# A hybrid encoder layer on one core: VectorE and ScalarE in source order in all stages

## The chip, the cores and the metric

The kernel runs on one core of a Trainium2 chip. Five engines with a queue of instructions each take part: TensorE (PE, matrix products), VectorE (DVE, elementwise work), ScalarE (ACT, activations, copies and casts), GpSimd (POOL) and SyncE (SP, which issues most of the DMA transfers). The metric is the device time of one execution in microseconds, lower is better. The kernel before took 1963.14 us, the median of three runs between 1960.15 and 1968.09.

## The reference

One encoder layer on a sequence of 1024 tokens of width 1024, all in float32. Each of three sub-layers is normalised ahead and behind (sandwich RMSNorm):

```
x += 1/2 * post(SwiGLU_1(pre(x)))                 # silu(x Wg) * (x Wu), then Wd; width 2816
x += post(W_out [ norm(NA heads) | norm(dilated heads) ])
x += 1/2 * post(SwiGLU_2(pre(x)))
```

The middle one has a combined projection to q, k and v for 16 heads of 64 elements. Eight heads do neighbourhood attention on a 16 x 64 grid of tokens, with a learned relative bias; eight do a mixture of three dilated sliding windows (128, 512 and 2048 wide, dilations 1, 4 and 16), merged with weights from the softmax denominators.

## The kernel before

**Products.** Each float32 operand is split into a high and a low part: ScalarE casts (`nc.scalar.copy(hi, raw)`, line 344) and VectorE subtracts (line 345). `mm3` (lines 251 to 253) makes one product of three TensorE passes, high by high, high by low, low by high. The GEMMs for gate and up (both FFNs) and for query and key are done by a scheme with seven products of half-size blocks (Winograd's form of Strassen's), named A11, A12, S2, S1, S3, S4 and A22 in the code. One product of a block is 12 matmuls. The down projections and the values take another form of the same scheme, in seven passes (`Passes`, with its own splits in lines 601 and 602). The output projection is plain.

**The loop of blocks.** `PairGemm.run` handles one block b of the weights per turn: 22 blocks in an FFN, 8 for query and key. For the first blocks (`early`: 9 in the first FFN, 10 in the second, all 8 for query and key) A11 and A12 were done in a phase before, `ahead`, and five products are left. In the source the turn of an early block holds, in this order:

- product S2, and VectorE adds u2 (line 470);
- the tail of the block before, `last()`: product A22, VectorE's c21 (line 507), the split of B22 (344 and 345, in `rest`), then the sink's work: Silu (554) and a product (555) for gate and up, and for every second block four more VectorE operations (563 to 566); for query and key `put`, which scales (806) and casts (808) on ScalarE and subtracts (809) on VectorE;
- the preparation of the next block's weights: `direct` (three VectorE operations, lines 432 to 434, ahead of them a split of the left weights where the next block isn't early) and `second` (the split of T2);
- product S1, and VectorE's v (line 478), which reads the bank of S1;
- product S3, c22 (line 499), the split of T1;
- product S4, which adds into the bank that v has read, and the sink's `second`.

A late block does all seven products. There s1, u2 and v are copies by ScalarE (line 363, in `keep`), the sink's `first` (VectorE's add 526, Silu 528) follows product A12, and `direct`, `second`, S1 and v follow that.

**What sets the order.** The instructions of a stage are handed to a scheduler. Within `ordered(*more)` it keeps TensorE in the order of the source, and the engines given as `more` too; for the others it chooses an order by its own costs. Before the change only the first stage (the first norm and the first products, up to `order.close()` in `begin`, line 1341) names VectorE and ScalarE. `c.behind(f, engines)` asks that f's instructions on these engines come no earlier than their place in the source. SP and POOL, and with them most DMA issues, are ordered by the scheduler everywhere.

**Three regions** follow the first stage: from line 1342 on, the rest of the first FFN, the value passes and query and key; from 1454, attention (`DilPair.head` and `na_head`) with parts of the output projection as fillers; from 1495, the output projection, its norms and the second FFN.

Of the kernel before, what the change touches and what calls it, by code (L numbers as in the profile page):

```python
# [16 lines left out]
SP, POOL, DVE, ACT = [getattr(mybir.EngineType, e) for e in ("SP", "Pool", "DVE", "Activation")]  # L17
# [822 lines left out]
def q_by_residue(c, copy, st):  # L840
    q = c.op.tile([P, SEQ], F32R, tag="q", name="q")
    by_residue(copy, q, st[:, 0])
    return q
# [264 lines left out]
def layer(tc, a, out):  # L1108
    nc = tc.nc
    c = Ctx(tc)  # L1110
    with ExitStack() as ctx:
        def pool(name, bufs, stack=ctx, **kw):
            return stack.enter_context(tc.tile_pool(name=name, bufs=bufs, reuse_waits="tile", **kw))

        def sub():
            return ctx.enter_context(ExitStack())
# [5 lines left out]
        def ordered(*more):  # L1122
            return tc.manual_schedule(engines={mybir.EngineType.PE, *more})
# [147 lines left out]
        def load_head():  # L1271
            if not heads:
                return
            p, hd = heads.pop(0)
            st = load_stack(c, p, hd)
            if hd == 0:
                pairs[p] = DilPair(c, p, attended if p == 2 * NP - 1 else lambda: None) if p >= NP else na_v(c, p)
            loaded.append((pairs[p], st, pairs[p].bias(hd) if p >= NP else na_bias(c, p, hd)))
# [15 lines left out]
        with ExitStack() as order:  # L1294
# [4 lines left out]
            def load(ts, queues):  # L1299
                for t, q in zip(ts, queues):  # L1300
                    xs[t] = c.xp.tile([P, D], F32, tag="x", name="x", bufs=4)
                    q.dma_start(xs[t], x0[t])
# [4 lines left out]
            def begin(pg):  # L1307
                load((2, 3), (nc.scalar, nc.sync))

                def drain():  # L1310
                    while c.sums:
                        c.sums.popleft()()

                def norm(*ts):
                    op0.scale(*n[ts])
                    drain()
                def junk():
                    return c.xp.tile([P, D], F32, tag="s", name="junk", bufs=2)
                n = {(0, 1): op0.squares([0, 1], [xs[0], xs[1]], junk())}
                norm(0, 1)  # L1320
                pg.split_left(0)
                n[2, 3] = op0.squares([2, 3], [xs[2], xs[3]], junk())
                op0.one(0)
                op0.one(1)
                pg.split_left(1)
                acc, s1 = [pg.bank() for _ in range(2)], []
                for b in range(2):
                    pg.mm(acc[b], pg.w[b], 0, A11, cols=slice(0, 256))
                op0.one(0)
                norm(2, 3)  # L1330
                op0.one(2)
                op0.one(3)
                for b in range(2):
                    pg.mm(acc[b], pg.w[b], 0, A11, cols=slice(256, 512))
                    s1.append(pg.save(b, acc[b]))
                    if b:
                        op0.one(1)
                load((4, 5), (nc.gpsimd, nc.gpsimd))
                op0.one(2)
                op0.one(3)  # L1340
                order.close()
                order.enter_context(ordered())
                return s1
            F = lambda *ts: lambda: op0.norm(ts, [xs[t] for t in ts])
            L, U = (lambda *ts: lambda: load(ts, [nc.gpsimd] * 2)), (lambda t: lambda: op0.put(t))
# [103 lines left out]
        def most():  # L1449

            early.extend(GroupNorm(c, og[0], 4 * quad, gd[:, :512], True, None) for quad in range(2))
            for n in early:
                c.todo.append(lambda n=n: c.behind(lambda: n.squares(slice(0, 448), 0), ACT))
        with ordered():
            ops = sub()
            c.op = pool("op", 2, ops)
            c.vp.append(c.op)
            load_head()
            qs = deque()

            def next_ready():

                if loaded:
                    d, st, g = loaded[0]
                    if isinstance(d, DilPair):
                        qs.append(q_by_residue(c, nc.gpsimd.tensor_copy, st))
                        by_residue(nc.gpsimd.tensor_copy, g[:, 0], g[:, 2])
                    else:
                        nc.gpsimd.tensor_add(g[:, 1], g[:, 0], c.cmask)
            c.behind(lambda: qs.append(q_by_residue(c, nc.scalar.copy, loaded[0][1])), ACT)  # L1470
            for p in range(NP, 2 * NP):
                for hd in range(2):
                    d, st, g = next_head()
                    if hd == 0:
                        d.outputs()
                    d.head(hd, st, qs.popleft(), g, next_ready, (1, 0) if p > NP or hd else (0, 1))
            c.left = 64
            for p in range(NP):
                for hd in range(2):
                    vs, st, nb = next_head()  # L1480
                    if (p, hd) == (NP - 1, 1):
                        c.todo.extend([lambda: None, most])
                    na_head(c, p, hd, og[0], vs, st, nb, next_ready, last if (p, hd) == (NP - 1, 1) else lambda q: None)
            c.last_units()
            c.fill(len(c.fillers))
            c.tick(len(c.todo))
            on = [c.xt.tile([P, 2, 4, T], F32R, tag=f"o{h}", name=f"n{h}") for h in (0, 2)]
            for n in early:
                n.ot = on
                c.steps.extend(lambda i=i, n=n: n.put(i) for i in range(4))  # L1490
# [1 line left out]

        s6 = sub()
        c.psm = pool("psm", 6, s6, space=PSUM)
        with ordered():
            part, ws, od = [xo[k] for k in ("part", "ws", "dil")]
            held = [nat_bank(c) for _ in range(4)]
            for t in range(4):
                for k in range(4):
                    nat_mm(c, held[t], od[1], t, k, ws, True, False)  # L1500
                    if t > 1 or k % 2:
                        c.step()
            c.flush()
            s4.close()
            s3.close()
            s2.close()
            c.xa = pool("xa", 1, side="right")
            prep = sub()
            hs1p = pool("hs1", 1, prep, side="right")
            p2, g3 = prep_pool(prep, [(a["mix_post_g"], "post"), (a["ffn2_pre_g"], "pre")])  # L1510
            left_pool(prep, side="right")
            op = Operand(c, g3, 2)
            pg = gate_pairs(3, op, a["wg2"], a["wu2"], 10)
            fin = Finish(c, x1, x2, p2, op)
            hs = [part, hs1p.tile([P, 4, D], F32, name="hs")]
            A = lambda *ts: lambda: fin.rest(ts, lambda t: hs[t // 4][:, t % 4, :])
            U = lambda t: lambda: op.put(t)

            def sink(h, t, g, ps):
                cols = slice(g * T, (g + 1) * T)  # L1520
                to = hs[h][:, t, cols]
                if h == 0:
                    nc.vector.tensor_add(to, ps, to)
                    ps = to
                sumsq(c, ps, fin.ss[:, 4 * h + t, g:g + 1])
                nc.vector.tensor_mul(to, ps, p2[:, cols])
                c.tick()
            for g in (1, 0):
                ws = nat_weights(c)
                for t in range(4):  # L1530
                    acc = nat_bank(c)
                    nat_chain(c, acc, on[0], t, ws, True, True)
                    sink(0, t, g, acc)
            plan(12, {0: [lambda: fin.scale(0, 4), A(0, 1)], 3: [A(2, 3)], 5: [U(0)], 6: [U(1)],
                      8: [lambda: queued(pg.start)], 9: [U(2)], 10: [U(3)]})
            for t in range(4):
                nat_chain(c, held[t], on[1], t, ws, False, True)
                sink(1, t, 0, held[t])
            ws, held = nat_weights(c), [nat_bank(c) for _ in range(4)]
            for t in range(4):  # L1540
                nat_chain(c, held[t], od[1], t, ws, True, False)
                c.tick()
            ws = nat_weights(c)
            for t in range(4):
                nat_chain(c, held[t], on[1], t, ws, False, True)
                sink(1, t, 1, held[t])
            c.flush()
            s1.close()
            s6.close()
            s7.close()  # L1550
            gemm_psum(ctx)

            ffn(3, op, prep, pg, get2,
                {0: [lambda: fin.scale(4, 4), A(4, 5)], 3: [U(4)], 4: [U(5), A(6, 7)], 7: [U(6)], 8: [U(7)]},
                down_sums(a["wd2"], ts2), [], a["ffn2_post_g"], None, x2, o)
            c.flush()
# [44 lines left out]
```

## Time and profile before

The profiled execution took 1962.61 us, of which the profile's span covers 1960.8; its mean granted TensorE clock was 0.981 of full speed.

| what | busy us | share of the span |
|---|---|---|
| TensorE matmuls (9044) | 1873.9 | 96% |
| TensorE weight loads, beside the matmuls | 1560.7 | 80% |
| VectorE (2235 instructions) | 1329.1 | 68% |
| ScalarE (1463) | 807.9 | 41% |
| GpSimd (520) | 323.3 | 16% |
| DMA, mean rate | 203 GB/s | |

In a row of the timeline stand the start and the duration in us, the engine, the line, the operation and its tiles (output first), the shapes, and in brackets the idle time of the engine just before with what ended it. In a row of windows each engine's busy time in that stretch is followed by its number of instructions, then come the granted TensorE clock, the mean share of busy DMA engines and the rate. In a row of waits stand the engine and line that waited, what it waited for, and the total in us, the number of times and the longest. Matmul records overlap: a matmul's duration is longer than the step from one to the next.

### The profile page before, as it was taken

To read this page: it belongs to the slowest core of one execution; us is meant where nothing else is said; L and a number is where in the kernel's file an instruction comes from. 1 tells how busy PE (TensorE), PEld (TensorE's weight loads), DVE (VectorE), ACT (ScalarE), POOL (GpSimd) and SP (SyncE) were. 2 spreads that over 40 slices of the span, in tenths; PEclk is the share of its full clock that TensorE was granted. 3 is DMA by queue.
4 is the path that set the end of the run, shared out by engine and by line. 5 is a ranking of instruction groups with operands and counts; after the bars stand their busy time and mean duration, and the time that the engine had idled before them with its cause. 6 is when DMAs were issued, how large, how long until landed. Compare 5 with 4: busy or idle time off the path is not lost.

```text
span 1960.8 us, 25563 instructions
## 1 busy us (share of the span) xinstructions
PE 1873.9 (96%) x9044; PEld 1560.7 (80%) x9044; DVE 1329.1 (68%) x2235; ACT 807.9 (41%) x1463; POOL 323.3 (16%) x520
## 2 busy tenths in 40 slices
PE   5999999999999999999899788998999999999997
PEld 4788888888888778778899777877888888888886
DVE  5778776765656785567566565676788767755567
ACT  4522333333534454133676555454222333345333
POOL 2101111111000123323434220021011111110000
PEclk8999999999999999999999899999999999999999
DMA  6645565547876667758999980375456665476663
GB/s 234 218 170 178 179 235 195 209 164 250 311 251 205 235 242 266 227 195 243 213 191 166 158 160 26 133 272 206 160 179 203 237 220 189 165 251 228 202 226 139
DMA packets 170433, 398.63 MB, mean 203 GB/s; under 512 B 20080, under 2 KB 41504, under 8 KB 170304
## 3 DMA queue, kind: packets, MB, share of 16 engines
q1 hardware_dynamic: 118800, 222.34, 36.2%
q0 software_dynamic: 50640, 172.55, 27.7%
q10 hardware_dynamic: 864, 2.10, 0.3%
q8 instruction: 71, 1.16, 0.2%
q14 instruction: 58, 0.48, 0.1%
HBM read 272.55 MB, written 127.26 MB: 204 GB/s over the span
## 4 chain that ended last, share of the span: by engine, by line
PE 82%; DMA 7%; DVE 6%; ACT 2%; issue 2%; SPq 1%; POOL 0%; DVEq 0%; ACTq 0%; POOLq 0%
PE mmp L253 17%; PE mmp L252 17%; PE mmp L251 17%; PE accp L251 8%; PE accp L252 8%; PE accp L253 8%; PE trp L159 2%; DMA vs<-v 1%; PE ptp L858 1%; PE po L1052 1%; DMA st<-qk 1%; DMA obn<-ob 1%; PE po L952 1%; DMA wraw<-in_wqk_dram 1%; PE sp L1035 1%
## 5 line engine op out<-in xcount | busy, mean ns | idle before, releaser
L251 PE MATMUL mmp<-x,whi 128*128 128x512 f32 (+1 forms) x1464 | 581.0, 397 | 7.5 <-ACT whi L344 3.5
L253 PE MATMUL mmp<-x,wlo 128*128 128x512 f32 (+1 forms) x1464 | 576.2, 394 | 1.1 <-DVE wlo L345 1.1
L252 PE MATMUL mmp<-x,whi 128*128 128x512 f32 (+1 forms) x1464 | 575.8, 393 | 0.5 <-DVE x L161 0.2
L251 PEld LDWEIGHTS mmp<-x,whi 128*128 128x128 f32 x1464 | 278.7, 190 | 67.7 <-ACT whi L344 4.2
L253 PEld LDWEIGHTS mmp<-x,wlo 128*128 128x128 f32 x1464 | 278.6, 190 | 62.6 <-DVE wlo L345 1.9
L252 PEld LDWEIGHTS mmp<-x,whi 128*128 128x128 f32 x1464 | 279.1, 191 | 59.8 <-DVE x L161 1.4
L602 DVE TENSOR_TENSOR pw<-praw,pw 128x1024 fp32r<-128x1024 f32 (+1 forms) x182 | 199.0, 1137 | 122.3 <-ACT pw L601 122.2
L601 ACT CAST pw<-praw 128x1024 fp32r<-128x1024 f32 (+1 forms) x182 | 168.9, 982 | 207.5 <-PE accp L253 170.1
L344 ACT CAST whi<-wraw 128x1024 fp32r<-128x1024 f32 x129 | 135.2, 1051 | 249.4 <-PE mmp L252 221.8
L251 PE MATMUL accp<-pw 128*128 128x512 f32 x600 | 234.2, 390 | 0.0
L253 PE MATMUL accp<-pw 128*128 128x512 f32 x600 | 233.5, 389 | 0.0
L252 PE MATMUL accp<-pw 128*128 128x512 f32 x600 | 233.4, 389 | 0.0
L345 DVE TENSOR_TENSOR wlo<-wraw,whi 128x1024 fp32r<-128x1024 f32 x129 | 157.6, 1224 | 24.3 <-ACT whi L344 24.1
L253 PEld LDWEIGHTS accp<-pw 128*128 128x128 f32 x600 | 112.6, 188 | 23.7
L252 PEld LDWEIGHTS accp<-pw 128*128 128x128 f32 x600 | 112.7, 188 | 23.1
L251 PEld LDWEIGHTS accp<-pw 128*128 128x128 f32 x600 | 112.6, 188 | 23.0
L549 POOL DMA_DIRECT2D g<-sg x44 | 23.8, 541 | 473.0 <-DVE sg L542 285.5
L507 DVE TENSOR_TENSOR c<-mmp,u 128x512 f32<-128x512 f32 x52 | 35.9, 691 | 82.6 <-PE mmp L253 82.6
L363 ACT COPY s<-mmp 128x512 f32<-128x512 f32 x52 | 30.5, 586 | 148.0 <-PE mmp L253 146.4
L344 ACT CAST whi<-traw 128x512 fp32r<-128x512 f32 x52 | 32.3, 621 | 117.7 <-DVE traw L433 59.0
L161 DVE TENSOR_TENSOR x<-trp,x 128x512 fp32r<-128x512 f32 x84 | 57.1, 686 | 34.4 <-ACT x L160 34.3
L432 DVE TENSOR_TENSOR wraw<-wraw 128x1024 f32<-128x1024 f32 x52 | 63.6, 1224 | 24.6 <-DMA wraw<-in_wqk_dram 14.3
(229 smaller groups left out, 2781.1 us busy)
## 6 DMA issues: line engine op xcount, KB each, us to landing
praw<-g SPq DMA_DIRECT2D x70, 512.0 KB
wraw<-in_wg_dram SPq DMA_DIRECT2D x44, 512.0 KB
wraw<-in_wu_dram SPq DMA_DIRECT2D x44, 512.0 KB
tr<-in_wd_dram SPq DMA_DIRECT2D x44, 512.0 KB
g<-sg POOLq DMA_DIRECT2D x88, 256.0 KB, 3.7
ts<-tr POOLq DMA_DIRECT2D x22, 1024.0 KB, 4.7
praw<-ts SPq DMA_DIRECT2D x88, 256.0 KB
praw<-in_wd_dram SPq DMA_DIRECT2D x66, 256.0 KB
```

The lines of the kernel that those rows point to most:

```text
L159: nc.tensor.transpose(ps[:, j, :], x[:, j * P:(j + 1) * P], c.ident)
L161: nc.vector.tensor_sub(lo, ps, hi.bitcast(F32))
L251: nc.tensor.matmul(out, ahi, bhi, start=start, stop=False, skip_group_check=go_on)
L252: nc.tensor.matmul(out, ahi, blo, start=False, stop=False, skip_group_check=go_on)
L253: nc.tensor.matmul(out, alo, bhi, start=False, stop=stop, skip_group_check=go_on)
L344: nc.scalar.copy(hi, raw)
L345: nc.vector.tensor_sub(lo, raw, hi.bitcast(F32))
L363: self.c.nc.scalar.copy(s, ps)
L432: nc.vector.tensor_sub(r[:, 0:2], r[:, 1:3], r[:, 0:2])
L507: nc.vector.tensor_add(c21, d, u2)
L601: nc.scalar.copy(w[side][:, 0, :m], raw[:, :m])
L602: nc.vector.tensor_sub(w[side][:, 1, :m], raw[:, :m], w[side][:, 0, :m].bitcast(F32))
```

## The change

Three calls name two more engines. In the regions from line 1342, 1454 and 1495 the scheduler keeps the VectorE and ScalarE instructions in the order in which the source issues them, as it does for TensorE. No instruction is added, removed or altered; SP and POOL stay with the scheduler.

```diff
@@ -1339,7 +1339,7 @@
                 op0.one(2)
                 op0.one(3)
                 order.close()
-                order.enter_context(ordered())
+                order.enter_context(ordered(DVE, ACT))
                 return s1
@@ -1451,7 +1451,7 @@
             for n in early:
                 c.todo.append(lambda n=n: c.behind(lambda: n.squares(slice(0, 448), 0), ACT))
-        with ordered():
+        with ordered(DVE, ACT):
             ops = sub()
             c.op = pool("op", 2, ops)
@@ -1492,7 +1492,7 @@
         c.psm = pool("psm", 6, s6, space=PSUM)
-        with ordered():
+        with ordered(DVE, ACT):
             part, ws, od = [xo[k] for k in ("part", "ws", "dil")]
```

## The prediction

> **What bounds the kernel now.** I read the page's totals, its slices and its chain of waits first, then four stretches of 50 us by engine.
>
> ```profile
> span 1960.8 us, 25563 instructions
> PE 1873.9 (96%) x9044; PEld 1560.7 (80%) x9044; DVE 1329.1 (68%) x2235; ACT 807.9 (41%) x1463; POOL 323.3 (16%) x520
> PE   5999999999999999999899788998999999999997
> PE 82%; DMA 7%; DVE 6%; ACT 2%; issue 2%; SPq 1%; POOL 0%; DVEq 0%; ACTq 0%; POOLq 0%
> ...
> core 0: us, PE busy (x) PEld busy (x) DVE busy (x) ACT busy (x) POOL busy (x), PEclk, DMA share, GB/s
> 100.00:150.00 50.00, 50.00 (x220) 41.14 (x219) 38.84 (x52) 10.81 (x13) 4.33 (x8) 1.00 0.48 163
> 250.00:300.00 50.00, 50.00 (x219) 40.97 (x219) 36.52 (x44) 16.23 (x23) 6.60 (x11) 1.00 0.59 217
> 850.00:900.00 50.00, 50.00 (x221) 40.95 (x220) 39.97 (x50) 21.40 (x26) 14.43 (x22) 1.00 0.67 211
> 1100.00:1150.00 50.00, 39.41 (x244) 35.28 (x245) 35.93 (x114) 31.55 (x99) 14.38 (x18) 0.83 0.85 155
> ```
>
> TensorE sets the time. In the early blocks of a gate-and-up GEMM (100 to 150), its late blocks (250 to 300) and the query-and-key GEMM (850 to 900) it never stops; only attention (1100 to 1150, nine slices of 49 us) leaves it idle, 10.59 of 50 us. Wherever TensorE is full, a new order of the other engines has nothing to gain, and costs time as soon as an operation that TensorE waits for stands behind one that it doesn't. So the question of each stage is: which instruction does the source put ahead of the one that TensorE needs next?
>
> **Early blocks (five products).** TensorE's order is S2, A22 of the block before, S1, S3, S4. S4 adds into the bank that v (line 478) reads, so S4 waits for v. In the source v stands behind the whole tail of the block before (line 507, the split of B22, line 555, in every second block 563 to 566) and behind the next block's weights (432 to 434 and T2's split). The rows show the scheduler's order, an even and an odd tail:
>
> ```profile
> 113.22 0.69 DVE L507 TENSOR_TENSOR c<-mmp,u 128x512 f32<-128x512 f32 x1 [1.46 <-PE mmp L253]
> 115.22 0.68 DVE L555 TENSOR_TENSOR c<-c,c 128x512 f32<-128x512 f32 x1
> 115.94 0.69 DVE L478 TENSOR_TENSOR v<-mmp,u 128x512 f32<-128x512 f32 x1
> ...
> 126.94 0.69 DVE L507 TENSOR_TENSOR c<-mmp,u 128x512 f32<-128x512 f32 x1 [1.36 <-PE mmp L253]
> 129.71 0.69 DVE L563 TENSOR_TENSOR s<-c,c 128x512 f32<-128x512 f32 x1
> 131.64 0.69 DVE L565 TENSOR_TENSOR sg<-s,sg 128x512 f32<-128x512 f32 x1
> 132.36 0.69 DVE L566 TENSOR_TENSOR sg<-sg 128x512 f32<-128x512 f32 x1
> ```
> ```profile
> 118.47 0.39 PE L251 MATMUL mmp<-x,whi 128*128 128x512 f32 x1
> ```
>
> v now runs at 115.94 and S4's first matmul at 118.47, which is 118.47 - 113.22 = 5.25 us after line 507 (S1 and S3 take that). The next weights take, where they run in a row:
>
> ```profile
> 247.76 0.69 DVE L526 TENSOR_TENSOR sg<-mmp,s 128x512 f32<-128x512 f32 x1
> 249.91 1.22 DVE L432 TENSOR_TENSOR wraw<-wraw 128x1024 f32<-128x1024 f32 x1
> ...
> 252.61 0.69 DVE L345 TENSOR_TENSOR wlo<-traw,whi 128x512 fp32r<-128x512 f32 x1
> 253.22 0.68 DVE L499 TENSOR_TENSOR c<-mmp,v 128x512 f32<-128x512 f32 x1
> ```
>
> From line 432's start to the start of what follows T2's split: 253.22 - 249.91 = 3.31 us. Even tail: line 432 can start 0.61 behind line 555, at 115.83; v starts 119.14, ends 119.83; S4, due at 118.47, is 1.4 late. Odd tail: the three dependents of line 563 follow at 0.72 each (132.36 - 131.64), so line 566 starts at 131.87, line 432 at 132.51, v at 135.82, and it ends 136.51; S4 was due at 126.94 + 5.25 = 132.19, so 4.3 late. The transfers of the weights are not late in either. Nine even tails (four in the first FFN with nine early blocks, five in the second with ten): 9 x 1.4 = 12.6. Eight odd ones: 8 x 4.3 = 34.4. The iteration ahead of the first late block also splits that block's left weights, one more operation of line 432's shape (1.22, of which some 0.1 overlaps its neighbour), 1.1 us, in each FFN: 2.2. Together 49.2 us. What is late next? c22 and T1's split have all of S4, S2 and A22 to catch up in, so each block starts again from zero, and the stalls add.
>
> **Late blocks (seven products).** Here v is a ScalarE copy (line 363), behind T2's cast in the source, and Silu (528) stands ahead of the cast of the left weights.
>
> ```profile
> 247.57 1.05 ACT L344 CAST whi<-wraw 128x1024 fp32r<-128x1024 f32 x1 [2.00 <-PE mmp L252]
> 248.53 0.63 ACT L528 ACTIVATE sg<-sg 128x512 f32<-128x512 f32 x1
> 250.49 0.59 ACT L363 COPY v<-mmp 128x512 f32<-128x512 f32 x1 [1.33 <-PE mmp L253]
> 251.96 0.62 ACT L344 CAST whi<-traw 128x512 fp32r<-128x512 f32 x1 [0.88 <-DVE traw L433]
> ```
> ```profile
> 253.00 0.39 PE L251 MATMUL mmp<-x,whi 128*128 128x512 f32 x1
> ```
>
> Silu waits for line 526, which ends at 248.45; some 0.55 later the cast starts, at 249.0 in place of 247.57: all behind it moves by 1.4. T2's cast then starts at 253.4, v at 253.9, and ends at 254.5. S4 was due at 253.0: 1.5 late. 12 such blocks in the first FFN (blocks 9 to 20) and 11 in the second: 23 x 1.5 = 34.5 us. If the cast keeps its place, T2's cast alone ahead of v ends at 252.6, and nothing is late: the bounds are 0 and 34.5. I take the upper, since the source has Silu first.
>
> **Query-and-key GEMM.** All eight blocks are early ones; the tail is `put`, casts on ScalarE and line 809 twice.
>
> ```profile
> 863.79 0.70 DVE L507 TENSOR_TENSOR c<-mmp,u 128x512 f32<-128x512 f32 x1
> ...
> 866.24 1.08 DVE L809 TENSOR_TENSOR qk<-c,qk 128x512 fp32r<-128x512 f32 x1 [0.62 <-ACT qk L808]
> 867.24 0.68 DVE L809 TENSOR_TENSOR qk<-qk 128x512 fp32r<-128x512 f32 x1
> 867.83 0.68 DVE L478 TENSOR_TENSOR v<-mmp,u 128x512 f32<-128x512 f32 x1
> 868.73 0.69 DVE L499 TENSOR_TENSOR c<-mmp,v 128x512 f32<-128x512 f32 x1 [0.21 <-PE mmp L253]
> ```
>
> Line 507 to the end of the tail: 867.83 - 863.79 = 4.04. S4 is due at 868.5 (line 499 waited for S3's end), line 507 could start at 868.5 - 5.25 = 863.25, so line 432 starts at 867.29, v at 870.60 and ends at 871.3: 2.8 late. Where the block before is one of neighbourhood attention, both line 809s take 0.68: 2.4. Six iterations prepare a next block behind a tail: 4 x 2.8 + 2 x 2.4 = 16.0 us.
>
> So the loops lose 49.2 + 34.5 + 16.0 = 99.7 us in 17 + 23 + 6 = 46 stalls.
>
> **The clock.** A stall of TensorE can cost more than itself:
>
> ```profile
> 845.03 0.50 PE L251 MATMUL mmp<-x,whi 128*128 128x512 f32 x1 [1.98 <-DVE c L499]
> ...
> 845.57:848.98 3.41, 3.41 (x9) 2.65 (x8) 1.09 (x2) 1.12 (x1) 1.45 (x2) 0.50 0.30 99
> 1094.00:1098.00 4.00, 2.54 (x22) 2.54 (x22) 0.78 (x3) 0.59 (x3) 1.47 (x3) 1.00 1.18 170
> ...
> 1095.46 0.48 PE L1035 MATMUL sp<-st 128*128 128x256 f32 x2 [1.57 <-DMA st<-qk]
> ```
>
> After a gap of 1.98 us the granted clock was 0.50 for 3.41 us, with 9 matmuls in place of some 15 (220 in 50 us); after one of 1.57 it stayed at 1.00. A halved window costs 3.41 / 2 = 1.7 us. The eight odd stalls and the six of the query-and-key GEMM lie above 1.98: 14 x 1.7 = 23.8. The 1.4s lie below. The late 1.5s lie by the edge: between 0 and 23 x 1.7 = 39, and as the nearest row had none, I take three, 5 us. [...]
>
> **The rest.** Waits of TensorE that the scheduler's own order makes, and the weights of the value passes:
>
> ```profile
> PE sp L1035 <- DVE stt L848: 7.3, 5, 2.3
> PE accp L252 <- DVE pw L602: 4.8, 4, 2.9
> PE mmp L251 <- DVE c L499: 2.0, 1, 2.0
> ```
> ```profile
> 687.91 0.15 DVE L132 TENSOR_TENSOR v<-fss 128x4 f32<-128x4 f32 x1
> ...
> 698.89 1.22 DVE L602 TENSOR_TENSOR pw<-praw,pw 128x1024 fp32r<-128x1024 f32 x1
> ```
>
> The second and third come where a split of later weights was put ahead and had to wait for its transfer; source order puts it back: -4.8 - 2.0 and two halved windows, -10.2. In the value passes the fourth weight tile's split (698.89) stands in the source ahead of the norm that started at 687.91 and would follow up to 11 us later; its buffer comes free only as TensorE goes on. Bounds 0 and 12; I take 5 and a window, 6.7. For attention and the output projection no row shows the new order: below, -7.3 (the first wait goes); above, +40, which is TensorE's idle share there, 10.59 of 50 us over 441 us or 93 us, growing by under half. Copies of one unit that stand behind the exponentials of the next speak for a loss; I take +15. Sum 11.5, between about -17 and +42.
>
> **Sum.** 99.7 + 23.8 + 5 + 11.5 = 140. On the profiled execution's span of 1960.8 with 1.8 outside it (1962.6, 0.5 below the median of the runs shown): 2102.6, **2103 us**.
>
> **Rivals.**
> *The late swap hides* (2063 us): the late blocks' cast is ready before Silu needs ScalarE, and 34.5 + 5 go. For it: ScalarE is busy only 16.23 of 50 us there. Against: a queue in order is stopped by one wait, however idle it is.
> *The late stalls halve the clock too, and attention pays* (2162 us): 39 - 5 = 34 more for windows, and 25 for attention, to its bound of 40.
> *Nothing measurable* (1963 us): v is not in fact held up, because what the source orders only binds among ready work, or the region is hardly reordered. For it: VectorE has 11 free us of 50. Against: in the first stage, which runs in source order already, the rows follow the source.
> *Faster* (1943 us): the loops keep step, and the waits on hoisted splits go. The place is the borders between stages and the score matmuls: 7.3 + 4.8 + 2.0 and three halved windows, 19.2 us. It decides if the 46 stalls together stay below 19.2, 0.4 us each; the smallest that I work out is 1.4, so this needs each of them wrong.
>
> **Chances.** Forecast 0.52 (its own range 2080 to 2130), late swap hidden 0.20, clock and attention 0.15, nothing measurable 0.07, faster 0.03, and 0.03 for something between 1973 and 2040. The range 2040 to 2170 leaves out the last three and a tail. A measurement of this kernel tells a change from none at about 0.5%, 9.8 us: faster 0.03, same 0.07, slower 0.90.
>
> **What will show it.** In a profile of the changed kernel TensorE's waits should have a row for VectorE's v (line 478) of 23 times and about 65 us, the longest over 4, and one for ScalarE's copy (363) with some 23 times at 1.5. In the early window v must come behind T2's split. If 100 to 150 us still shows TensorE full, the first step is wrong, and with it the forecast. The granted clock should fall below 1.00 in early stretches and remain near it in late ones; if late stretches show 0.9, the second rival is right. Attention's share is wrong if its stretch shifts by more than 40 us.

## The result and the profile after

The changed kernel takes 2161.97 us (median, 2158.64 to 2165.09) against 1962.01 for the kernel before beside it: a ratio of 1.1013, 95% interval 1.0983 to 1.1043. It is 200 us slower. The profiled execution's span is 2163.3 us, 202.5 longer than before.

The totals and TensorE's slices on the page of the changed kernel:

```profile
span 2163.3 us, 25505 instructions
PE 1942.7 (90%) x9044; PEld 1592.5 (74%) x9044; DVE 1345.2 (62%) x2235; ACT 801.0 (37%) x1463; POOL 323.3 (15%) x520
PE   5988899999999889988999788988888999999997
```

VectorE and ScalarE do the same work in the same number of instructions. TensorE's busy time grew by 1942.7 - 1873.9 = 68.8 us with the same 9044 matmuls, and the other 134 us are idle time. By the clock's record in the two profiles TensorE was busy at half clock for 58 us before and for 160 us after; half of the difference, some 51 us of the 68.8 by this estimate, is the clock's. The rest isn't traced here. Windows of the changed kernel, in an early stretch, a late one and the query-and-key loop:

```profile
100.00:150.00 50.00, 43.95 (x183) 35.05 (x182) 33.89 (x43) 9.33 (x12) 4.58 (x9) 0.97 0.42 142
250.00:300.00 50.00, 47.24 (x197) 37.83 (x195) 32.94 (x40) 13.34 (x19) 6.02 (x11) 0.96 0.47 168
950.00:1000.00 50.00, 41.75 (x164) 33.24 (x163) 33.20 (x40) 16.26 (x20) 11.15 (x18) 0.90 0.49 160
```

TensorE did 183, 197 and 164 matmuls in 50 us where it had done 219 to 221. What TensorE waited for (total, times, longest):

```profile
PE mmp L251 <- DVE v L478: 65.2, 26, 5.5
PE mmp L251 <- ACT v L363: 32.0, 23, 1.7
PE trp L159 <- DVE xn L200: 23.2, 3, 11.8
PE po L1052 <- ACT pt L860: 20.4, 13, 4.7
...
PE accp L252 <- DVE wlo L117: 6.3, 4, 2.8
...
PE mmp L251 <- ACT u L363: 5.8, 2, 2.9
```

The first two rows are the stalls ahead of S4; neither is among the waits of the kernel before. The third was 18.5 us there.

**Where the 202.5 us come from.** TensorE executes the same matmuls in the same order in both kernels, so the nth matmul of one can be set against the nth of the other. The starts of fifteen such matmuls (the first and the last of a stage, or near them), in us from the start of each span, and the growth of the distance from line to line:

```
TensorE has reached                        before     after   distance   grown
first FFN: start of the block loop         107.48    110.25       2.77     2.8
  end of the early blocks                  219.97    256.91      36.94    34.2
  end of the late blocks                   451.25    508.40      57.15    20.2
  last block's S4                          465.01    527.02      62.01     4.9
down projection, well under way            632.76    694.77      62.01     0.0
  its last pass                            653.67    719.89      66.22     4.2
query and key: second block                853.12    934.35      81.23    15.0
  end of its loop                          928.74   1035.32     106.59    25.4
attention: end                            1243.26   1366.09     122.83    16.2
output projection: end                    1290.40   1425.93     135.53    12.7
second FFN: start of the block loop       1392.32   1531.14     138.81     3.3
  end of the early blocks                 1506.56   1681.07     174.51    35.7
  end of the late blocks                  1719.96   1913.19     193.23    18.7
  last block's S4                         1736.03   1933.98     197.95     4.7
down projection: last matmuls             1949.80   2151.74     201.94     4.0
```

The block loops cost 34.2 + 20.2 + 25.4 + 35.7 + 18.7 = 134.2 us, their last blocks 9.6, everything else 58.7.

**The stalls themselves.** VectorE's timeline of the changed kernel, an even and an odd tail, and S4's first matmul behind each:

```profile
118.03 0.68 DVE L555 TENSOR_TENSOR c<-c,c 128x512 f32<-128x512 f32 x1
118.63 1.22 DVE L432 TENSOR_TENSOR wraw<-wraw 128x1024 f32<-128x1024 f32 x1
...
121.93 0.68 DVE L478 TENSOR_TENSOR v<-mmp,u 128x512 f32<-128x512 f32 x1
...
136.30 0.69 DVE L566 TENSOR_TENSOR sg<-sg 128x512 f32<-128x512 f32 x1
136.91 1.22 DVE L432 TENSOR_TENSOR wraw<-wraw 128x1024 f32<-128x1024 f32 x1
...
140.20 0.68 DVE L478 TENSOR_TENSOR v<-mmp,u 128x512 f32<-128x512 f32 x1
```
```profile
122.76 0.47 PE L251 MATMUL mmp<-x,whi 128*128 128x512 f32 x1 [1.37 <-DVE v L478]
...
141.03 0.51 PE L251 MATMUL mmp<-x,whi 128*128 128x512 f32 x1 [4.27 <-DVE v L478]
...
141.50:145.00 3.50, 3.50 (x11) 2.71 (x10) 1.29 (x2) 0.00 (x0) 0.00 (x0) 0.54 0.23 94
```

From line 432's start to v's start it is 121.93 - 118.63 = 3.30 and 140.20 - 136.91 = 3.29 us. Behind the longer stall the granted clock is 0.54. In a late block, ScalarE's timeline and S4's first matmul:

```profile
287.14 0.63 ACT L528 ACTIVATE sg<-sg 128x512 f32<-128x512 f32 x1 [2.91 <-DVE sg L526]
287.68 1.03 ACT L344 CAST whi<-wraw 128x1024 fp32r<-128x1024 f32 x1
...
292.04 0.62 ACT L344 CAST whi<-traw 128x512 fp32r<-128x512 f32 x1 [3.33 <-DVE traw L433]
292.57 0.58 ACT L363 COPY v<-mmp 128x512 f32<-128x512 f32 x1
```
```profile
293.20 0.50 PE L251 MATMUL mmp<-x,whi 128*128 128x512 f32 x1 [1.38 <-ACT v L363]
```

Silu (line 528) now runs ahead of the left weights' cast, where it ran behind it before; so line 433 comes later, T2's cast waits for line 433, and v stands behind T2's cast. ScalarE was free for 3.33 us before that cast and could not use them for v.

### The profile page after: what moved, and what is told of

The parts are those of the page before. It is cut to its first block, busy times and chain, and to the rows that moved or that the text cites. A ratio compares the mean times of both kernels' runs of the same rounds, so it can differ in the third digit from the quotient of the medians.

```text
span 2163.3 us, 25505 instructions
## 1 busy us (share of the span) xinstructions
PE 1942.7 (90%) x9044; PEld 1592.5 (74%) x9044; DVE 1345.2 (62%) x2235; ACT 801.0 (37%) x1463; POOL 323.3 (15%) x520
## 5 line engine op out<-in xcount | busy, mean ns | idle before, releaser
L251 PE MATMUL mmp<-x,whi 128*128 128x512 f32 (+1 forms) x1464 | 596.8, 408 | 108.9 <-DVE v L478 65.2
L253 PE MATMUL mmp<-x,wlo 128*128 128x512 f32 (+1 forms) x1464 | 586.6, 401 | 2.9 <-DVE wlo L345 2.9
L252 PE MATMUL mmp<-x,whi 128*128 128x512 f32 (+1 forms) x1464 | 586.4, 401 | 0.6 <-DVE x L161 0.4
L251 PEld LDWEIGHTS mmp<-x,whi 128*128 128x128 f32 x1464 | 285.2, 195 | 190.2 <-ACT whi L344 77.8
L253 PEld LDWEIGHTS mmp<-x,wlo 128*128 128x128 f32 x1464 | 284.6, 194 | 68.3 <-DVE wlo L345 4.6
L252 PEld LDWEIGHTS mmp<-x,whi 128*128 128x128 f32 x1464 | 285.0, 195 | 60.9 <-DVE x L161 1.5
L160 ACT CAST x<-trp 128x512 fp32r<-128x512 f32 x84 | 48.7, 586 | 83.4 <-PE trp L159 83.3
```

What stands on the lines that cost most here:

```text
L160: nc.scalar.copy(hi, ps)
L251: nc.tensor.matmul(out, ahi, bhi, start=start, stop=False, skip_group_check=go_on)
L252: nc.tensor.matmul(out, ahi, blo, start=False, stop=False, skip_group_check=go_on)
L253: nc.tensor.matmul(out, alo, bhi, start=False, stop=stop, skip_group_check=go_on)
```

## The experiments

The theory: in the loops it is the place of v in the source, on VectorE in early blocks and on ScalarE in late ones, and the rest comes from other places where an operation that TensorE waits for stands late in the source. The main rivals: that two queues in source order can't keep TensorE fed whatever the source; that stalls of 2.0 to 2.8 us, as in these runs, leave the clock alone; and that the 59 us outside the loops come from what the loops leave behind.

**One engine at a time.** All three regions, first VectorE alone in source order, then ScalarE alone.

```diff
-                order.enter_context(ordered(DVE, ACT))
+                order.enter_context(ordered(DVE))      # and ordered(ACT)
...
-        with ordered(DVE, ACT):
+        with ordered(DVE):                             # and ordered(ACT), both places
```

> VectorE alone in source order, ScalarE left to the scheduler as before. Theory (the early and the query-and-key stalls come from VectorE's order, the late ones from ScalarE's): TensorE's waits on v of line 478 stay (26 waits, 65 us), those on the copies of line 363 (23 of 1.4 us for v and the last block's two of 2.9 for u2) go. By the difference of TensorE's matmuls between the two profiles the early loops cost 34 + 37 us and query and key 25, so 1962 + 97 = 2059 us, and up to 57 us more, as much of what lies outside the loops as is VectorE's: 2059 to 2116. Rival (both engines' order is needed for either stall): below 2000 us, or the late stalls stay.

> ScalarE alone in source order. Theory: the late stalls stay (23 of about 1.5 us, 39 us with what follows) and the last block's (10 us), the early ones go: 1962 + 49 = 2011 us, and up to 57 more: 2011 to 2068. Rival (the late stall comes from VectorE's line 526, which Silu waits for, in source order): the late stalls go, and the time is below 2000 us.

VectorE alone: 2108.2 us (ratio 1.0745, 1.0723 to 1.0766). ScalarE alone: 2053.9 us (1.0468, 1.0447 to 1.0489). TensorE's first wait in each, VectorE's order first:

```profile
PE mmp L251 <- DVE v L478: 73.4, 26, 5.8
```
```profile
PE mmp L251 <- ACT v L363: 31.9, 23, 1.5
```

Each order keeps its own stall and loses the other's. By the same setting of matmul against matmul, VectorE's order costs the first FFN's early blocks 34.6 us and the late ones 0.0; ScalarE's 6.4 (one stall of 4.5 us as the late blocks begin, with its window) and 20.2. In attention ScalarE's order costs 17.7 us and VectorE's 3.8, so attention's loss is mostly ScalarE's; the output projection loses under either (12.5 and 9.6). The two losses, 146 and 92 us, exceed the 200 of both together, since several places are paid once for either.

**The loop's source rearranged, everything in source order.** v moves ahead of the operations that TensorE doesn't wait for; TensorE's own order is unchanged.

```diff
@@ PairGemm.run, early block
...
-                if last:
-                    last()
-                direct()
-                second()
+                done = last() if last else None      # A22, c21, split of B22
                 a = self.bank()
                 self.mm(a, w[T1], 0, S1)
                 v = sp.tile([P, T], F32, tag="v", name="v")
                 nc.vector.tensor_add(v, a, u2)
+                left()                               # split of the next left weights
+                direct()
+                second()
+                pairs = done() if done else None     # sink.last; lines 563 to 566 behind sums()
@@ late block
...
+                left()
                 self.sink.first(b, pb, False, s1)
+                if final and b == self.n - 1:
+                    final()                          # was ahead of S2
                 direct()
-                second()
                 self.mm(a, w[T1], 0, S1, True)
                 v = self.keep(a, "v")
+                second()
```

> All three regions in source order as in the changed kernel, but the source of the block loop is rearranged: v stands ahead of the next block's weights, the tail of the block before and T2's split; the left weights' split ahead of Silu; the first splits of the down projection behind Silu in the last block. TensorE's order is untouched. Theory (the position in the source is the whole cause in the loops): of the 200 us, 135 in the loops and 10 in the last blocks go, 55 us outside stay: 2017 us, and TensorE is full in 100 to 150, 250 to 300 and 900 to 950 us. Rival (a queue in source order can't keep TensorE fed, because VectorE with 41 of 50 us... is nearly full and every wait adds up): stalls of 0.5 us or more remain in most blocks, over 2060 us.

2027.3 us (ratio 1.0334, 1.0317 to 1.0351), 10 above the expectation; the profiled execution, the fastest of four, took 2022.4. Windows of this kernel in the same three stages:

```profile
100.00:150.00 50.00, 50.00 (x221) 41.07 (x220) 39.40 (x51) 12.09 (x16) 4.86 (x9) 1.00 0.50 170
250.00:300.00 50.00, 50.00 (x220) 40.96 (x219) 37.80 (x47) 17.20 (x24) 6.77 (x12) 1.00 0.63 235
900.00:950.00 50.00, 50.00 (x222) 41.42 (x221) 40.42 (x53) 20.75 (x28) 17.81 (x28) 1.00 0.87 247
```

TensorE is full again, with both engines in source order. Against the kernel before, the distance grows by 0.0 in the first FFN's block loop up to its last block, by 0.0 to 0.1 in the second's, and by 0.4 and 0.6 in the last blocks. The rival of queues that can't keep up is refuted. (The 41 of 50 us that it gives for VectorE are the weight loads' figure; VectorE has 38.84 in the early row before and 39.40 here.) In the profiled execution 59 us remain outside the loops, 4 more than expected.

**How long a stall must be for the clock to fall.** The changed kernel, with v copied once, twice or three times in the late blocks.

```diff
                 v = self.keep(a, "v")
+                for _ in range(b % 3):
+                    nc.scalar.copy(v, a)
```

> The changed kernel, with ScalarE's copy to v in the late blocks made once, twice or three times (block number modulo 3), each some 0.5 us; the output is the same. It lengthens the late stall from 1.5 to about 2.1 and 2.6 us, eight blocks each. Theory of the clock (a gap of TensorE over some 1.7 to 2 us is followed by 3.41 us at half clock): a block with two copies loses 0.5 + 1.7 more than one with one, with three 1.1 + 1.7 more: about 8 x 2.2 + 7 x 2.8 = 37 us over the changed kernel. [...]

2202.7 us in one run, 41 us above the changed kernel's median and 37.6 above its profiled execution. Set against the changed kernel's matmuls, a block with two copies starts S4 0.62 us later and one with three 1.18 later (0.91 in one), and behind 14 of these 16 stalls another 1.5 to 1.6 us are lost within some twenty matmuls. Two stalls of one length, and the windows behind them:

```profile
296.19 0.50 PE L251 MATMUL mmp<-x,whi 128*128 128x512 f32 x1 [2.00 <-ACT v L497]
...
296.50:300.50 4.00, 4.00 (x19) 3.25 (x18) 2.84 (x4) 0.59 (x1) 0.26 (x1) 1.00 0.05 22
...
362.31 0.57 PE L251 MATMUL mmp<-x,whi 128*128 128x512 f32 x1 [2.00 <-ACT v L497]
...
362.50:366.00 3.50, 3.50 (x9) 2.75 (x9) 1.71 (x2) 0.71 (x1) 0.00 (x0) 0.51 0.00 0
```

Behind the second the clock is 0.51, behind the first 1.00; the last section has what set two equal gaps of the changed kernel apart. The loss is the theory's size; the longer stalls by themselves come to 14 us (8 x 0.62 + 7 x 1.18 + 0.91).

**Source order in the loops alone, source not rearranged.** The order is switched to VectorE and ScalarE as a block loop begins and back behind it, in both FFNs and around the query-and-key loop.

```diff
+            switch(DVE, ACT)        # closes the open ordered(...) and enters this one
             pg.run(final)
+            switch()
```

> The kernel before, with VectorE and ScalarE in source order only while a block loop runs, and the loop's source not rearranged. Theory (the loops' order alone carries 135 + 10 of the 200 us, and the run with the rearranged loop gained 11): 1963 + 145 - 11 = 2097 us, between 2090 and 2107. Rival (source order in the loops hurts only together with the order of the stages around them): below 2060 us.

2091.4 us (ratio 1.0654, 1.0623 to 1.0684), in the theory's interval: the loops do it alone.

**The rearranged loop, with source order only there.** Both edits above together.

> The rearranged block loop of the run before, with VectorE and ScalarE in source order only while a block loop runs (both FFNs, query and key); value passes, attention, output projection, the phases ahead of the loops and the down projections are left to the scheduler, as in the kernel before. Theory (what was left, 55 us, is made by the order of those other stages, and the loops cost nothing now): all of it goes, and the gap of 1.98 us at the start of the query-and-key loop with its halved window, 3.9 us, goes too: 1958 us. Rival (part of the 55 us comes from what the loops leave behind at their borders): over 1970 us.

1951.4 us; ratio 0.9938, 0.992 to 0.9956. This is faster than both kernels, by some 12 us against the one before. Its TensorE reaches the second query-and-key block 9.8 us earlier than that kernel's; the wait of 1.98 us at 845 us is gone, and so is the longest of those on line 602 (2.89 at 807), and it keeps 8.3 us to the end. In the kernel before, the scheduler had put the loop's preparation of its second block of weights into the value passes, ahead of a split of theirs on line 602, and VectorE waited there for the transfer:

```profile
803.76 1.23 DVE L432 TENSOR_TENSOR wraw<-wraw 128x1024 f32<-128x1024 f32 x1 [6.18 <-DMA wraw<-in_wqk_dram]
```

The run with the source not rearranged has no such row there either and gained as much on the same stretch (9.6 us); in the block loops of the FFNs the distance grows by about 0.1 us at most here. So the gain comes from switching the order at the query-and-key loop, which keeps its work out of the value passes, and the rearranging only keeps the loops from losing. Whether the order itself gives it or the border between stages that the switch sets was not tested. All of the 59 us go as well, so they come from the order of the other stages and not from the loops' borders.

**The rearranged loop, order left to the scheduler.** The control for the one before.

> The rearranged block loop with the order of VectorE and ScalarE left to the scheduler in all stages behind the first, as in the kernel before. Theory (the source's order counts only where it is followed): within 0.3% of the kernel before, 1957 to 1968 us. Rival (the scheduler takes the source's order as a preference, so that the rearranged source is itself what helps): off by more than 6 us.

1962.0 us; ratio 0.9997, 0.9981 to 1.0012. The rearranged source by itself does nothing; it counts where it is followed.

**Attention given back to the scheduler**, all else in source order with the loop rearranged.

> As the rearranged kernel in source order, but attention left to the scheduler. Theory: the 23 us that the attention stage costs by the difference of TensorE's matmuls go, no other stage moves: 2027 - 23 = 2004 us. Rival (the value passes, the output projection or the fillers between are what delays attention): above 2015 us.

2007.0 us (ratio 1.0219, 1.019 to 1.0249), 20 us below the 2027.3 with attention in source order. Set matmul against matmul, attention's loss against the kernel before falls from 21.3 to 4.3 us. So nearly all of it comes from attention's own order, as the theory had it.

**Two lower bounds beside the loops' order.**

```diff
-            pg.begin()
-            pg.begin_rest()
+            c.behind(pg.begin, DVE, ACT)
+            c.behind(pg.begin_rest, DVE, ACT)
@@ Weights.next
-            nc.scalar.copy(hi, raw)
-            nc.vector.tensor_sub(lo, raw, hi.bitcast(F32))
+            c.behind(lambda: (nc.scalar.copy(hi, raw), nc.vector.tensor_sub(lo, raw, hi.bitcast(F32))), DVE, ACT)
```

> As the kernel with source order in the block loops alone, and in the other stages two lower bounds on the scheduler's choice: the first query-and-key weights' preparation and the splits of the output projection's weights come no earlier on VectorE and ScalarE than their place in the source. Theory (two of TensorE's waits in the kernel before come from such operations put ahead while their transfer is under way: 4.8 us at 807 us of its profile and 4.0 at 1176, halved windows included): 1958 - 9 = 1949 us. Rival (the waits only move to what is then late, as with the splits of the output projection in source order, which cost 10 us there): 1958 us or more.

1959.9 us (ratio 0.9977, 0.9964 to 0.999): slower than with the loops' order alone. The wait in attention at 1176 us did go (3.5 us), but in the output projection 11.9 us are lost against the kernel before, where the weights' splits now come late (TensorE waits 1.17, 1.74 and 1.26 us for them). The time is in the rival's interval.

**One long chain of attention in three pieces.**

```diff
...
-            scales = [lambda n=n: c.behind(n.scale, DVE) for n in norms]
+            scales = [lambda f=f: c.behind(f, DVE) for n in norms for f in n.thirds()]
```

> The rearranged kernel in source order in all stages, with the norm of each half of the dilated heads' output issued in three turns (1/root, rows 0 and 1, rows 2 and 3) in place of one turn of 13 + 4 VectorE operations, some 5.2 us in a row. Theory (in attention a long chain in one turn holds up the score reductions behind it, which cost 3.3 and 3.9 us and a halved window each): the two waits fall below 2 us, 5 to 8 us go: 2027 - 7 = 2020 us. Rival (the work holds TensorE up by its amount, not by its length in one piece): within 3 us of 2027.

2023.6 us (2018.9 to 2027.6), against 2027.3 (2022.4 to 2028.3) for the kernel with the chain whole: not told apart. The waits on line 860 (873 in these two kernels), chain whole, then in thirds:

```profile
PE po L1065 <- ACT pt L873: 21.8, 15, 4.3
```
```profile
PE po L1065 <- ACT pt L873: 23.7, 17, 4.9
```

The two waits did fall below 2 us, as the theory had it (3.31 and 3.86 to 1.17 and 1.62), and TensorE gains 8 us there; but the next wait is one of 4.87, which takes 5 of them within 15 us, and none is left as the output projection begins. In this run the work held TensorE up at its new places as well; whether it would anywhere in a fixed order wasn't tested. Which order of attention would do as well as the scheduler's stays open.

## Why the prediction was right, and where it fell short

The direction, the cause and the place were right, and 2162 lies in the range of 2040 to 2170, but above the likeliest case's own range of 2080 to 2130. The forecast of 2103 was 59 us low. That the range holds 2162 is in part luck: the sum with its own bounds for "the rest" ends at 1962.6 + 128.5 + 42 = 2133, and beyond that lies only a rival whose mechanism did not come about.

**The early stalls** were forecast at 1.4 and 4.3 us; the rows above have 1.37 and 4.27, and 3.30 us for the weights where 3.31 had been taken. The late stall was forecast at 1.5; it waits 1.38 and costs 1.7 per block (20.2 / 12), so that the late blocks' 38.9 came near the forecast 34.5 + 5 without the windows in it. Query and key were forecast at 16.0 and 10.2 for the clock; 25.4 was measured. In all, the loops were put at 99.7 + 28.8 = 128.5 us and cost 134.2. The late stalls did come, as ScalarE's order alone showed, so the rival in which they hide is out.

**The clock** was right in kind. No stall of 1.4 us in the loops is followed by a halved window, all eight odd ones are, so the three late windows that I allowed for (5 us) weren't there. (The late window's 0.96 is the end of the half clock behind the early stall at 249 us.) What was low is the odd ones' price: four of them were followed by 3.41 us at half clock and lost 1.6 to 1.7 us by it, four by twice that time, and these lost 2.4 to 2.9, where one window had been put at 1.7. Of the six long stalls of query and key one, of 2.74 us at 975, halved nothing.

**The step that failed is "the rest"**, put at 11.5 us between -17 and +42. It measured 202.5 - 134.2 = 68.3, beyond these bounds. Of this:

- 9.6 us are the last blocks of the two loops, which the prediction left out. The source issues the first splits of the down projection (`final`) ahead of u2, and S1 adds into the bank that u2 reads:

```profile
518.24 1.04 ACT L601 CAST pw<-praw 128x1024 fp32r<-128x1024 f32 x1 [1.79 <-DMA praw<-in_wd_dram]
519.19 0.58 ACT L363 COPY u<-mmp 128x512 f32<-128x512 f32 x1
```
```profile
519.82 0.50 PE L251 MATMUL mmp<-x,whi 128*128 128x512 f32 x1 [2.94 <-ACT u L363]
```

  In the rearranged loop, where `final` follows Silu, 1.0 of the 9.6 is left.
- The value passes lost 15.0 net where 6.7 - 10.2 was forecast. The mechanism that was named (the fourth tile's split ahead of the norm) was there:

```profile
767.68 1.23 DVE L602 TENSOR_TENSOR pw<-praw,pw 128x1024 fp32r<-128x1024 f32 x1 [6.70 <-ACT pw L601]
768.82 0.15 DVE L132 TENSOR_TENSOR v<-fss 128x4 f32<-128x4 f32 x1
```
```profile
779.01 1.09 PE L159 MATMUL trp<-ident,xn 128*128 128x128 f32 x4 [6.38 <-DVE xn L200]
```

  The norm starts 768.82 - 687.91 = 80.9 us later than before, where the transposes' place in TensorE's order is 70 later, so it lost 11, as bounded (the matmul just ahead of the wait started at 702.59 before and 772.25 after). TensorE waited 6.38 us for it here, and from there to 805 us the distance grows by some 9.5 us, where 6.7 had been taken. More was lost where the prediction looked for nothing: TensorE waited for the casts of line 601 at 753.55 (3.46 us, 3.9 of distance) and at 851.72, where the distance grows by 6.7 with the clock:

```profile
849.48 0.60 ACT L803 ACTIVATE qk<-mmp 128x512 f32<-128x512 f32 x1 [2.21 <-DMA qk<-qk]
```
```profile
851.72 0.79 PE L251 MATMUL accp<-pw,x 128*128 128x512 f32 x1 [2.95 <-ACT pw L601]
```

  On ScalarE the cast stands behind line 803, which waited for a transfer. Smaller losses make up the rest (2.7 near 903, 1.1 near 820). The gains came nearly as forecast: 4.8 us on the way to line 602's products and 3.9 at the start of the query-and-key loop, 8.7 for 10.2.
- Attention and the output projection lost 16.2 + 12.7 = 28.9, where 15 was taken inside bounds to +40. An example of attention's, in the changed kernel:

```profile
1211.42 2.00 DVE L1001 TENSOR_TENSOR og<-oa,obn 128x1024 f32<-128x1024 f32 x1 [2.67 <-POOL oa L998]
1213.34 0.54 DVE L848 CUSTOM_DVE_ANT_0 sb<-sp,nb 128x384 f32<-128x384 f32 x1
```
```profile
1215.01 1.11 PE L1052 MATMUL po<-vs,pt 128*128 128x64 f32 x4 [4.70 <-ACT pt L860]
```

  The score reduction (848) stands behind a sum that waits for GpSimd, the exponential behind the reduction, and ScalarE's copy of the transposed block behind the exponential: one wait crosses three queues.
- The first phase ahead of a loop (2.8), the second (3.3) and the two down projections' ends (4.2 and 4.0) were counted as nothing or not at all; 0.6 lies behind the last matmuls.

**The rival at 2162 us** gave the measured time to the microsecond for reasons that weren't so: none of the late stalls of 1.4 to 1.7 us halved the clock, and attention with the output projection lost 28.9 and not 40. **Nothing measurable** and **faster** are out; what speaks for the second is that a part of its gains exists: 8.3 us are left at the end where the loops are rearranged and alone in source order.

## What to carry to other kernels

A queue in source order is as good as the source: ahead of the instruction that the bounding engine needs next, count everything that the source issues on that queue, and the waits of each. Put the operation that frees an accumulating bank directly behind the product that fills it, and preparation for later behind it; then a fixed order can match a scheduler's in a regular loop, as here in the first FFN's, where the distance to the kernel before grew by 0.0 us in place of 54.4 (34.2 + 20.2). Ask it stage by stage: here a fixed order kept to the rearranged loops gained 11 us (1962.0 to 1951.4), nearly all of it ahead of the second query-and-key block, where the loop's work had been put into the stage before it and waited for a transfer, and it cost 76 in the other stages (1951.4 to 2027.3).

## What the runs showed of the hardware that was not expected

In the run with copies a gap of TensorE of 2.00 us was followed by half clock at 362 us (0.51 from 362.50 to 366.00) and not at 296 us (1.00 from 296.50 to 300.50) of one execution. Of eight such gaps seven were, of eight of 2.56 us seven, of twenty-three late ones of 1.4 to 1.7 us in the changed kernel none. So in these runs the length mattered, but it didn't decide alone.

What else went with it can be worked out from the profiles of the kernel before and of the changed one, from their changes of the clock and the gaps between matmuls. In each of these two executions all changes of the clock (25 and 65) are whole multiples of 3.413 us apart, to within 0.002 us: half clock begins at 141.32, 175.45 and 213.00 in the changed kernel, 10 and 11 steps apart. Add up TensorE's idle time within each such step that ran at full clock, from 45 us on. After 1.9 us or more of idle time in a step the next was halved in all of 38 cases (9 before, 29 after), after less than 1.3 us in none of 1035; between these it was halved in 5 of 37. Two gaps of 2.74 us in the changed kernel's query-and-key loop differ in this. The one that ended at 957.32 has 2.53 us in the step up to 957.11, and the clock was 0.50 from there to 960.52; the one that ended at 975.44 is split at 974.17, into 1.47 and 1.27, and the clock stayed at 1.00 up to 981.00. So in these two executions it was the idle time in one step that went with the halving, and a gap's place on the grid was luck for the kernel. The matmuls' ends are modelled, so the idle times and both limits are estimates.

And one gap can cost more than one window: of the eight odd stalls of the changed kernel's early blocks (seven of 4.27 us, one of 5.53) four go with 3.41 us at half clock and four with 6.83, and they lost between 1.6 and 2.9 us behind them.
